# The layer-input gate as seven half-block products for each pair of token tiles

## Chip, cores and metric

The kernel runs on one core of a Trainium2 chip. The metric is device time in microseconds (us) of one execution: the median of several runs. A profile is one execution of its own, recorded by the hardware profiler; its span runs from the first instruction of the program to the last.

## What is computed

One layer of a streaming encoder in float32: 1024 prompt tokens and 8 x 16 sample tokens, which together are nine tiles of 128 tokens, with 1024 features each. Attention and the SwiGLU feed-forward come first and are not touched. The change concerns the end:

```python
    x = x + mix @ w_out
    h = rmsnorm(x, g_ffn)
    x = x + (jax.nn.silu(h @ w_gate) * (h @ w_up)) @ w_down      # w_down is 2816 x 1024
    gate = jax.nn.sigmoid(rmsnorm(x, g_ple) @ w_ple_gate)        # w_ple_gate is 1024 x 1024
    x = x + gate * (p @ w_ple_proj)
    return x, new
...
    y_prompt = rmsnorm(xp, g_final)
    y_sample = rmsnorm(xs, g_final)
```

The product `p @ w_ple_proj` is made much earlier and lies in DRAM (`proj`). The layer-input gate is the 1024 x 1024 product under the sigmoid.

## The kernel before, in words

**Numbers.** Each float32 operand is split in a high part (a cast to the matmul's reduced float32) and a low part (the difference). `mm3` makes one product of three matmuls: high by high, high by low, low by high. The cast is made by ACT, the difference by DVE or POOL (`sub`, L111). So 128 tokens by 128 features by n columns cost three matmuls of n columns.

**Queues and order.** Every DMA is issued by SP, in one in-order queue, in which an issue that waits holds up all behind it. The order of the instructions on each engine is made by the framework's scheduler; inside `tc.manual_schedule(engines=...)` an engine keeps the order in which the code is written.

**Down projection.** Ten of the eleven blocks of 256 rows of `w_down` are done in `nd = 5` iterations of 512 rows (`for d in range(nd)`). Tiles t and t + 4 form a pair; the two tiles by two halves of the features are a 2 x 2 block matrix, and `forms` makes the sums of blocks with which seven products do the work of eight. `raws(d)` loads an iteration's inputs one iteration ahead: `actr` (activations), `sr` (sums of activations, made earlier and kept in DRAM), `wr` and `wraw` (weights). `put` splits them in `acth`/`actl` (low part on POOL) and `whi`/`wlo` (low part on DVE); `plus` makes sums of weights (`t`, `wr`). `times` (L1307) is the products, `onto` (L1312) adds a bank of PSUM to the residual rows `x1[t]`. The eleventh block is left to `down`: for each tile t two halves of 512 columns, 12 matmuls, and an add (L1418). Before it, POOL adds twelve half rows `u2` onto `x1` (L1414).

**Gate.** `close(t)`, run after each tile's `down`, makes tile t's normalized row `hrow` (squares on ACT, L197; the power on POOL, L117; scaled by `g_ple` on DVE, L199), turns tile t - 1's row with eight transposes (L1452, out `pt`) and splits the result in `hVh` and `hVl`. `gate(c, w, t)` is one quarter of 256 columns for one tile: 24 matmuls of 256 columns (`mm3`, L106 to L108, out `ps` from `whi`/`wlo` and `hVh`/`hVl`), sigmoid (L1436), product with `pj` (L1437), add onto `x1` (L1438), squares for the last norm (L1439). Quarter 0 is interleaved with `down`; quarters 1 to 3 follow, each over nine tiles. In quarter 3 the final scale (L1479 to L1482) and the store of the tile follow. `wq`, `gated` and `wf` do not exist yet.

Of the kernel before, what the change touches and what calls it, by code (L numbers as in the profile page):

```python
# [13 lines left out]
F32 = mybir.dt.float32  # L14
F32R = mybir.dt.float32r
# [7 lines left out]
P = 128  # L23
D = 1024
# [15 lines left out]
def tile_hymba_step(  # L40
# [64 lines left out]
    def mm3(out, ah, al, bh, bl, start, stop):  # L105
        T.matmul(out, lhsT=ah, rhs=bh, start=start, stop=False)  # L106
        T.matmul(out, lhsT=ah, rhs=bl, start=False, stop=False)  # L107
        T.matmul(out, lhsT=al, rhs=bh, start=False, stop=stop)  # L108
# [48 lines left out]
    def cols(w, c, n=256):  # L157
        return w[:, c * n : (c + 1) * n].rearrange("(k p) c -> p k c", p=P)
# [50 lines left out]
    actd = [dram.tile([P, 2, NT * P], F32, name=f"act{i}") for i in range(DFF // 256)]  # L209
    actsd = [dram.tile([P, 3, 512], F32, name=f"acts{i}") for i in range(DFF // 256 - 1)]  # L210
    mixs = [dram.tile([P, 512], F32, name=f"mixs{i}") for i in range(2)]


    kv_prompt = {(0, 1): sb_k_p, (0, 2): sb_v_p, (1, 1): cb_k_p, (1, 2): cb_v_p}
# [504 lines left out]
    def pool(stack, name, side, bufs=1):  # L719
        return stack.enter_context(tc.tile_pool(name=name, bufs=bufs, side=side, reuse_waits="tile"))  # L720
# [243 lines left out]
    def bank(n=512):  # L964
        return ps_o.tile([P, 512], F32, name="ps", tag="O")[:, :n]
# [162 lines left out]
    with tc.tile_pool(name="ph4b", bufs=2, side="right", reuse_waits="tile") as p4b:  # L1128
# [200 lines left out]
    with tc.manual_schedule(engines={mybir.EngineType.SP}):  # L1329
        fetch_x1((0, 1, 2, 3, 8), 0)  # L1330
        fetch_x1((4, 5, 6, 7), 1)
        fetch_x1((0, 1, 2, 3, 8), 1)
        fetch_x1((4, 5, 6, 7), 0)
        ahead = raws(1)
    for d in range(nd):
# [68 lines left out]
    hT = Transposed()  # L1404
    for half in range(2):
        hT.add(pool(ctx, f"h5{half}", "left"), half, "hV")

    def down(w, act, last):
        for t in range(NT):
            s = slice(t * P, (t + 1) * P)  # L1410
            for half in range(2):
                o = slice(half * 512, half * 512 + 512)
                if t < NP and (t, half) > (3, 1) or t < 4 and half:
                    G.tensor_tensor(x1[t][:, o], x1[t][:, o], u2[t % 4], op=ALU.add)  # L1414
                ps_ = bank()
                for f in range(2):
                    mm3(ps_, act[f][0][:, s], act[f][1][:, s], w[0][:, f, o], w[1][:, f, o], f == 0, f == 1)
                V.tensor_tensor(x1[t][:, o], x1[t][:, o], ps_, op=ALU.add)  # L1418
            last(t)


    def gate_weights(c):
        return ch.load(cols(w_ple_gate[0], c), KT, 256, 2)

    p6 = pool(ctx, "ph6", "right", 2)
    ss = [p6.tile([P, 4], F32, name=f"ss{t}", bufs=1) for t in range(NT)]

    def gate(c, w, t):
        o = slice(c * 256, (c + 1) * 256)
        pj = p6.tile([P, 256], F32, name="pj", tag="pj", bufs=4)  # L1430
        nc.sync.dma_start(pj, proj[t * P : (t + 1) * P, o])
        ps_ = bank(256)
        for k in range(KT):
            mm3(ps_, *hT.tok(t, k), w[0][:, k], w[1][:, k], k == 0, k == KT - 1)
        sg = p6.tile([P, 256], F32, name="sgp", tag="sgp")
        A.activation(sg, ps_, AF.Sigmoid)  # L1436
        V.tensor_tensor(sg, sg, pj, op=ALU.mult)  # L1437
        (V if c == 3 else G).tensor_tensor(x1[t][:, o], x1[t][:, o], sg, op=ALU.add)  # L1438
        A.activation(sg, x1[t][:, o], AF.Square, accum_out=ss[t][:, c : c + 1])  # L1439

    def close(t):

        if t < NT:
            rows.append(normed(p6, x1[t], g_row, t))
        if t == 0:
            return
        h = rows.pop(0)
        for half in range(2):
            pt = tbank()
            for j in range(4):  # L1450
                c = (half * 4 + j) * P
                T.transpose(pt[:, j * P : (j + 1) * P], h[:, c : c + P], ident)  # L1452
            dh, dl = hT.dst(t - 1, half)
            A.copy(dh, four(pt))  # L1454
            sub(V, dl, four(pt), dh)
        if t > LATE:
            gate(0, w_g, t - 1 - LATE)

    w_g = gate_weights(0)
    g_row = load_row(gr, g_ple[0:1, :], "grow")  # L1460
    down(w_d, act, close)
    close(NT)
    for t in range(NT - LATE, NT):
        gate(0, w_g, t)


    gf_row = load_row(gr, g_final[0:1, :], "grow")
    for c in range(1, 4):
        w_g = gate_weights(c)
        for t in range(NT):  # L1470
            gate(c, w_g, t)
            if c == 2:
                part = p6.tile([P, 1], F32, name="part", tag="part", bufs=NT)
                V.tensor_reduce(part, ss[t][:, 0:3], axis=AX.X, op=ALU.add)
                V.tensor_scalar(ss[t][:, 0:1], part, 1.0 / D, EPS, op0=ALU.mult, op1=ALU.add)
                G.tensor_tensor(x1[t][:, :768], x1[t][:, :768], gf_row[:, :768], op=ALU.mult)
            if c == 3:
                r = p6.tile([P, 1], F32, name="r", tag="r", bufs=4)
                V.scalar_tensor_tensor(r, ss[t][:, 3:4], 1.0 / D, ss[t][:, 0:1], op0=ALU.mult, op1=ALU.add)  # L1479
                G.tensor_tensor(r, r, nhalf[:, 0:1], op=ALU.pow)  # L1480
                V.tensor_tensor(x1[t][:, 768:], x1[t][:, 768:], gf_row[:, 768:], op=ALU.mult)
                V.tensor_scalar(x1[t], x1[t], r[:, 0:1], None, op0=ALU.mult)  # L1482
                nc.sync.dma_start(y_tok[t], x1[t])


INPUTS = (
# [47 lines left out]
```

## Time and profile before

| | |
|---|---|
| median of 3 runs | 1732.53 us (1726.93 to 1733.93) |
| the profiled execution | 1727.71 us, its span 1725.6 us |
| busy share of the span | PE 97%, PEld 84%, DVE 61%, ACT 45%, POOL 45% |
| mean granted TensorE clock | 0.995 |
| stretch of the five iterations of the down projection | 1357 to 1571.5 us of the span |
| stretch of the last block, the transposes and the gate | 1571.5 to 1717.8 us |
| bytes moved by DMA | 279.40 MB |

How to read it: PE is TensorE's matmuls, PEld its weight loads, DVE VectorE, ACT ScalarE, POOL GpSimd, SPq the issue of a DMA by SP. A row of the timeline has the start in the span, the time taken, the engine, the line of the kernel, the operation, and "out<-in" by the program's names; in square brackets stands the idle time of the engine before it and who ended it. A row of groups has the count, the busy time of all, the mean of one in ns, and the idle time before them. A matmul's own duration is longer than the distance to the next one, since they overlap; a stretch and its count tell the rate. PEclk is the granted share of TensorE's clock.

### The profile page before, as it was taken

What the parts mean: (1) busy time and instruction counts of PE and PEld (TensorE: products, weight loads), DVE (VectorE), ACT (ScalarE), POOL (GpSimd) and SP (SyncE); (2) the same over time, 40 slices, a digit from 0 to 9 for tenths busy, and PEclk for the clock granted to TensorE, in tenths of its full rate; (3) what the DMA queues carried; (4) which work ended last, traced back from release to release, by engine and by line L of the source; (5) the groups of instructions that cost most, each with busy time, mean ns of one, the idle gap of its engine ahead of it and who ended that gap; (6) DMA issues with size and microseconds to landing.
All of it is one profiled execution on the core that took longest, in us unless ns stands there. A gap on an engine that the chain in (4) does not pass through costs nothing.

```text
span 1725.6 us, 29066 instructions
## 1 busy us (share of the span) xinstructions
PE 1668.2 (97%) x11076; PEld 1457.6 (84%) x11076; DVE 1044.9 (61%) x1640; ACT 776.4 (45%) x1698; POOL 774.3 (45%) x584
## 2 busy tenths in 40 slices
PE   8999999999997998899999999999999999999998
PEld 7998888889995887787778888888888788887998
DVE  5112344277778675654886666666666698887635
ACT  5214545276767776643643333333332343333432
POOL 2313301287446422222455555555554565558364
PEclk9999999999999999999999999999999999999999
DMA  5847898656469986855413222222222874311123
GB/s 191 278 145 226 287 293 284 189 171 184 119 176 267 296 252 185 232 165 176 142 56 115 88 87 90 95 95 95 95 95 95 291 292 136 120 39 61 59 71 141
DMA packets 172620, 279.40 MB, mean 162 GB/s; under 512 B 15297, under 2 KB 103617, under 8 KB 171074
## 3 DMA queue, kind: packets, MB, share of 16 engines
q1 hardware_dynamic: 172482, 277.55, 49.9%
q8 instruction: 88, 1.44, 0.4%
q14 instruction: 50, 0.41, 0.1%
HBM read 197.95 MB, written 79.56 MB: 161 GB/s over the span
## 4 chain that ended last, share of the span: by engine, by line
PE 86%; DMA 5%; DVE 3%; ACT 2%; issue 1%; POOL 1%; SPq 0%; POOLq 0%; ACTq 0%; DVEq 0%
PE ps L1056 20%; PE ps L106 9%; PE ps L107 9%; PE ps L108 9%; PE pt L1307 6%; PE ps L1307 4%; PE pt L1056 3%; PE pt L608 3%; PE pt L395 2%; PE po L632 2%; DMA mixn<-mixp 2%; PE acc L463 2%; PE po L631 2%; PE S L575 1%; PE sdec L418 1%; PE S L576 1%
## 5 line engine op out<-in xcount | busy, mean ns | idle before, releaser
L111 POOL TENSOR_TENSOR wlo<-wraw,whi 128x512 fp32r<-128x512 f32 (+1 forms) x127 | 224.4, 1794 | 205.6 <-ACT whi L150 201.7
L106 PE MATMUL ps<-whi,hTh 128*128 128x256 f32 x576 | 167.7, 291 | 0.1
L107 PE MATMUL ps<-wlo,hTh 128*128 128x256 f32 x576 | 164.2, 285 | 0.0
L108 PE MATMUL ps<-whi,hTl 128*128 128x256 f32 x576 | 163.9, 285 | 0.0
L150 ACT CAST whi<-wraw 128x512 fp32r<-128x512 f32 (+1 forms) x128 | 88.2, 753 | 94.1 <-PE ps L1056 64.8
L589 DVE TENSOR_TENSOR_SCAN keep<-keep,zero 128x128 f32<-128x128 f32 (+4 forms) x64 | 99.1, 1558 | 37.6 <-ACT keep L581 36.6
L590 POOL TENSOR_TENSOR w<-w,keep 128x127 f32<-128x127 f32 (+4 forms) x64 | 83.4, 1313 | 73.1 <-DVE keep L589 64.0
L106 PEld LDWEIGHTS ps<-whi,hTh 128*128 128x128 f32 x576 | 110.2, 191 | 6.0 <-issue 5.4
L108 PEld LDWEIGHTS ps<-whi,hTl 128*128 128x128 f32 x576 | 110.2, 191 | 0.5 <-DVE hTl L111 0.2
L107 PEld LDWEIGHTS ps<-wlo,hTh 128*128 128x128 f32 x576 | 110.3, 192 | 0.1
L111 DVE TENSOR_TENSOR wtl<-pt,wth 128x512 fp32r<-128x512 f32 (+1 forms) x192 | 94.2, 514 | 18.1 <-ACT wth L612 17.2
L612 ACT CAST wth<-pt 128x512 fp32r<-128x512 f32 (+1 forms) x192 | 84.4, 463 | 44.2 <-PE pt L608 43.4
L608 PE MATMUL pt<-ident,w 128*128 128x128 f32 x528 | 87.9, 278 | 5.5 <-POOL w L590 2.1
L106 PE MATMUL ps<-whi,hVh 128*128 128x256 f32 x288 | 81.9, 284 | 0.5 <-ACT hVh L1454 0.5
L107 PE MATMUL ps<-wlo,hVh 128*128 128x256 f32 x288 | 81.7, 284 | 0.0
L108 PE MATMUL ps<-whi,hVl 128*128 128x256 f32 x288 | 81.6, 284 | 0.0
L575 PE MATMUL S<-qk 128*128 128x384 f32 (+2 forms) x192 | 71.4, 373 | 5.8 <-ACT keep L581 3.9
L631 PE MATMUL po<-wth,vk 128*128 128x256 f32 (+1 forms) x304 | 76.3, 283 | 0.2
L608 PEld LDWEIGHTS pt<-ident,w 128*128 128x128 f32 x528 | 61.8, 141 | 15.4 <-issue 3.6
L632 PE MATMUL po<-wtl,vk 128*128 128x256 f32 (+1 forms) x304 | 72.7, 282 | 0.0
L111 POOL TENSOR_TENSOR actl<-actr,acth 128x1024 fp32r<-128x1024 f32 (+1 forms) x22 | 56.7, 2579 | 33.6 <-DMA sr<-acts 18.2
L106 PE MATMUL ps<-hTh,whi 128*128 128x384 f32 x192 | 66.0, 344 | 0.0
(359 smaller groups left out, 5335.9 us busy)
## 6 DMA issues: line engine op xcount, KB each, us to landing
draw<-in_cache_sb_k SPq DMA_DIRECT2D x32, 512.0 KB, 5.3
draw<-in_cache_sb_v SPq DMA_DIRECT2D x32, 512.0 KB, 5.1
act<-sg SPq DMA_DIRECT2D x11, 1152.0 KB
actr<-act SPq DMA_DIRECT2D x22, 576.0 KB, 5.4
wraw<-in_w_in SPq DMA_DIRECT2D x11, 1024.0 KB, 5.2
wraw<-in_w_gate SPq DMA_DIRECT2D x11, 1024.0 KB
wraw<-in_w_up SPq DMA_DIRECT2D x11, 1024.0 KB
v<-sv SPq DMA_DIRECT2D x36, 256.0 KB, 4.5
```

The lines of the kernel that those rows point to most:

```text
L106: T.matmul(out, lhsT=ah, rhs=bh, start=start, stop=False)
L107: T.matmul(out, lhsT=ah, rhs=bl, start=False, stop=False)
L108: T.matmul(out, lhsT=al, rhs=bh, start=False, stop=stop)
L111: eng.tensor_tensor(out, a, hi.bitcast(F32), op=ALU.subtract)
L150: A.copy(h[:, o], v[:, o])
L575: T.matmul(sc, lhsT=hd["qq"][:, qs], rhs=hd["kkh"][:, kc], start=True, stop=False)
L589: V.tensor_tensor_scan(rev, rev, zero[:, 0:1].to_broadcast([P, n]), 1.0, op0=ALU.mult, op1=ALU.add)
L608: T.transpose(pt[:, (c - c0) * P : (c - c0 + 1) * P], w[:, c * P : (c + 1) * P], ident)
L631: T.matmul(dst, lhsT=vs, rhs=wth[:, kb - base, c0:c1], start=(i == 0), stop=False)
L632: T.matmul(dst, lhsT=vs, rhs=wtl[:, kb - base, c0:c1], start=False, stop=(i == nkb - 1))
L1056: T.matmul(out, lhsT=a[x][:, k], rhs=b[y][:, k], start=(not more and k == 0 and n == 0), stop=(k == 3 and n == 2), skip_group_check=more)
L1307: T.matmul(out, lhsT=a[i][:, x, m * P : (m + 1) * P], rhs=b[j][:, x], start=(not more and x == 0 and n == 0), stop=(x == 1 and n == 2), sk ...
```

## The change

The gate's product is now made like the down projection's: for each pair (t, t + 4), A11, A12 are the halves of the features of tile t, A21, A22 those of tile t + 4, and seven products of half blocks (128 x 512 by 512 x 512 each) stand for eight. Tile 8, which has no partner, keeps the plain form. Parts:

- **Weights' sums beside the down projection.** `gate_sums(k)`, called in iterations d = 1 to 4 with k = d - 1, loads four 128 x 512 blocks of `w_ple_gate`, scales them by `g_ple` on ACT, makes four differences on POOL, and writes seven blocks to DRAM (`gated`). That is 16 loads, 16 ACT operations, 16 POOL operations and 28 stores of 256 KB.
- **Weights read back.** After the iterations, seven loads of 1 MB from `gated` go into the places of the buffers that the iterations leave (`wf`) and are split in place (`weights_parts`): W0, W2, W4 and the seventh with their low parts on DVE, W1, W3, W5 on POOL.
- **Tiles in the order** 0, 4, 1, 5, 2, 6, 3, 7, 8 in `down`; the twelve POOL adds stand ahead of them all.
- **`prepare(p)`** makes a pair's rows (no `g_ple` any more; scaled on ACT, on DVE for tiles 0, 4 and 8; one buffer `hrow` instead of two), turns them, and makes the sums and seven splits. PE's order from here to the end is written out by hand.
- **The pair loop**: seven products (12 matmuls of 512 columns each), into four banks, with adds on DVE (`u`, `u3`, `u4`), and four gates of 512 columns. Then tile 8 by 24 matmuls of 512 and 72 of 256 columns.
- `proj` comes in two rows of 1024 per pair in place of 36 loads of 256 columns; the final scale is one DVE operation on 1024 columns with both factors.

```diff
-    xr, gr = pool(ctx, "xr", "right"), pool(ctx, "gr", "right")
+    xr = pool(ctx, "xr", "right")
...
+    def gate_sums(k):
+
+        q = {}
+        for x in range(2):
+            for y in range(2):
+                q[x, y] = wq.tile([P, 512], F32, name=f"q{x}{y}", tag=f"q{x}{y}", bufs=1)
+                row = (x * 4 + k) * P
+                nc.sync.dma_start(q[x, y], w_ple_gate[0, row : row + P, y * 512 : y * 512 + 512])
+                A.activation(q[x, y], q[x, y], AF.Copy, scale=g_gate[:, x * 4 + k : x * 4 + k + 1])
...
+        for i, v in ((0, q[0, 0]), (1, q[1, 0]), (6, q[1, 1])):
+            out(i, v)
+        G.tensor_tensor(t3, q[1, 1], q[0, 1], op=ALU.subtract)
+        G.tensor_tensor(q[0, 1], q[0, 1], q[0, 0], op=ALU.subtract)
+        G.tensor_tensor(t2, q[1, 1], q[0, 1], op=ALU.subtract)
+        G.tensor_tensor(q[1, 0], q[1, 0], t2, op=ALU.subtract)
+        for i, v in ((2, t2), (3, t3), (4, q[0, 1]), (5, q[1, 0])):
+            out(i, v)
...
         S3, T3, A4, T4 = got
+        if d:
+            gate_sums(d - 1)
...
+    W = [own_place(i) for i in range(5)] + [ch.pair(4, 512)]
+    for i in range(6):
+        nc.sync.dma_start(W[i][1].bitcast(F32), gated[i])
+    b22 = ch.raw(gated[6], 4, 512)
...
-    def gate(c, w, t):
-        o = slice(c * 256, (c + 1) * 256)
...
-        for k in range(KT):
-            mm3(ps_, *hT.tok(t, k), w[0][:, k], w[1][:, k], k == 0, k == KT - 1)
...
+    weights_parts(0, V)
+    weights_parts(2, V)
+    for i, t in enumerate(tiles):
+        down(t, w_d, act)
+        if i == 1:
+            coming = prepare(0)
+            next(coming)
+            with tc.issue_after(pows[0].ins):
+                weights_parts(1, G)
+        if i == 4:
+            next(coming)
+            weights_parts(3, G)
+            weights_parts(5, G)
+        if i == 6:
+            forms_ = next(coming)
+            with tc.issue_after(last_split[0]):
+                weights_parts(4, V)
+    W.append(ch.parts(b22, 4, 512, 2, V))
...
+    for p in range(4):
+        A11, A12, S2, S3, S1, A22, S4 = forms_
...
+        product(a, A11, W[0])
+        A.copy(u, a)
...
+        product(b, S2, W[2])
+        V.tensor_tensor(u, u, b, op=ALU.add)
+        product(a, A12, W[1], True)
...
+        product(c, S3, W[3])
+        V.tensor_tensor(u3, u, c, op=ALU.add)
+        if p < 3:
+            next(coming)
...
+            gate(p, 0, 512, 0, a, G)
...
+        product(d, S1, W[4])
+        V.tensor_tensor(u3, u3, d, op=ALU.add)
+        gate(p + 4, 512, 512, 1, u3, G)
+        if p < 3:
+            forms_ = next(coming)
+        product(c, A22, W[5], True)
+        V.tensor_tensor(u4, u, c, op=ALU.add)
+        gate(p + 4, 0, 512, 0, u4, G)
+        close(p + 4, 2)
+        product(d, S4, W[6], True)
+        V.tensor_tensor(u, u, d, op=ALU.add)
+        gate(p, 512, 512, 1, u, G)
+        close(p, 2)
```

How this moves instructions, at three places. Line numbers after the change are those of the changed kernel: L1223 has become L1224, L1231 L1232, L1273 L1274, L1056 (`product`) L1057.

**SP, the loads for the fourth iteration of the down projection.** Before, these stand one behind the other (`actr` is that iteration's activations, `wraw` and `wr` its weights):

```order
L1223 DMA actr<-act_105 128x1152
L1223 DMA actr<-act_106 128x1152
L135 DMA wraw<-in_w_down 128x2x1024
L1223 DMA actr<-act_105 128x1152
L1223 DMA actr<-act_106 128x1152
L1231 DMA wr<-in_w_down 128x2x1024
```

And now (L1348 is a load of `gate_sums`, L1353 a store; `gated_120` to `gated_126` are the seven blocks):

```order
L1224 DMA actr<-act_105 128x1152
L1224 DMA actr<-act_106 128x1152
L1353 DMA gated_122<-t_16374 128x512
L1348 DMA q_16700<-in_w_ple_gate 128x512
L1348 DMA q_16706<-in_w_ple_gate 128x512
L1353 DMA gated_120<-q_16697 128x512
L135 DMA wraw<-in_w_down 128x2x1024
L1353 DMA gated_125<-q_16368 128x512
L1224 DMA actr<-act_105 128x1152
L1224 DMA actr<-act_106 128x1152
L1353 DMA gated_126<-q_16706 128x512
L1232 DMA wr<-in_w_down 128x2x1024
```

Four DMAs of `gate_sums` now stand between the first `actr` pair and `wraw`, one between `wraw` and the second pair, one between that and `wr`; each store waits for the ACT or POOL operation that makes its block.

**POOL, in the third iteration.** Before, from the first low part of that iteration's sums on:

```order
L111 TENSOR_TENSOR actl<-sr,acth 128x1024 x2
L1273 TENSOR_TENSOR t_15679<-wraw,t_15679 128x1024
L111 TENSOR_TENSOR actl<-sr,acth 128x1024
L111 TENSOR_TENSOR actl<-actr,acth 128x1024
L1273 TENSOR_TENSOR wr<-wraw,wr 128x2x512
L111 TENSOR_TENSOR actl<-actr,acth 128x1024 x3
```

Now, from one row further on (L1357 to L1360 are the differences of `gate_sums`):

```order
L1360 TENSOR_TENSOR q_16020<-q_16020,t_16026 128x512
L111 TENSOR_TENSOR actl<-sr,acth 128x1024
L1274 TENSOR_TENSOR t_15713<-wraw,t_15713 128x1024
L1357 TENSOR_TENSOR t_16375<-q_16371,q_16365 128x512
L111 TENSOR_TENSOR actl<-sr,acth 128x1024
L1358 TENSOR_TENSOR q_16365<-q_16365,q_16362 128x512
L111 TENSOR_TENSOR actl<-actr,acth 128x1024
L1359 TENSOR_TENSOR t_16374<-q_16371,q_16365 128x512
L1274 TENSOR_TENSOR wr<-wraw,wr 128x2x512
L1360 TENSOR_TENSOR q_16368<-q_16368,t_16374 128x512
L111 TENSOR_TENSOR actl<-actr,acth 128x1024 x2
```

The scheduler put the differences together: of the 16, counted from one iteration's last `d8l` to the next one's, 4 stand in the second iteration's list, 11 in the third's, 1 in the fourth's, none in the fifth's.

**PE, the gate.** Before, quarter 0 of the gate (`hV`, 256 columns), the last block's `down` (`act`, 512 columns) and the transposes stand mixed:

```order
L106 MATMUL ps<-whi,hVh_16701 128x256
L1452 MATMUL pt<-ident,hrow 128x128 x8
L107 MATMUL ps<-wlo,hVh_16701 128x256
L108 MATMUL ps<-whi,hVl_16702 128x256
L106 MATMUL ps<-whi,hVh_16701 128x256
```

Now each pair has its products of 512 columns, with the next pair's transposes ahead of and behind the product with W4 (its twelve matmuls are rows like the three shown):

```order
L1057 MATMUL ps<-W3h,actl 128x512
L1500 MATMUL pt<-ident,hrow 128x128 x8
L1057 MATMUL ps<-W4h,acth 128x512
L1057 MATMUL ps<-W4l,acth 128x512
L1057 MATMUL ps<-W4h,actl 128x512
```

After W4's twelve matmuls come the eight transposes of the pair's second tile. Both sets read the same single buffer `hrow`, so twelve matmuls lie between them.

More of the change, by code (lines that the diff above doesn't have):

```diff
@@ L211, in tile_hymba_step @@
     mixs = [dram.tile([P, 512], F32, name=f"mixs{i}") for i in range(2)]
+    gated = [dram.tile([P, 4, 512], F32, name=f"gated{i}") for i in range(7)]
     kv_prompt = {(0, 1): sb_k_p, (0, 2): sb_v_p, (1, 1): cb_k_p, (1, 2): cb_v_p}
@@ L1401, in tile_hymba_step @@
             onto(4 + m, 0, m7[m])
-    bstack.close()
[L1404 to L1419, printed above, removed]
@@ L1441, in close @@
[L1441 to L1449, printed above, removed]
-            for j in range(4):
[L1451 to L1483, printed above, removed]
@@ new lines, in tile_hymba_step, with weights_parts @@
+    tiles = [0, 4, 1, 5, 2, 6, 3, 7, 8]
+    for t in tiles[:-1]:
+        for half in range(2):
+            if t > 3 or half:
+                o = slice(half * 512, half * 512 + 512)
+                G.tensor_tensor(x1[t][:, o], x1[t][:, o], u2[t % 4], op=ALU.add)
+    bstack.close()
+    wf = pool(ctx, "wf", "left")
+    def weights_parts(i, eng):
+        hi, lo = W[i]
+        raw_ = lo.bitcast(F32)
+        for o in (slice(0, 2), slice(2, 4)):
+            A.copy(hi[:, o], raw_[:, o])
+            sub(eng, lo[:, o], raw_[:, o], hi[:, o])
@@ new lines, in own_place, with down @@
+    def own_place(i):
+        return [wf.tile([P, 4, 512], F32R, name=f"W{i}{n}") for n in "hl"]
+    W = [own_place(i) for i in range(5)] + [ch.pair(4, 512)]
+    for i in range(6):
+        nc.sync.dma_start(W[i][1].bitcast(F32), gated[i])
+    b22 = ch.raw(gated[6], 4, 512)
+    def down(t, w, act):
+        s = slice(t * P, (t + 1) * P)
+        for half in range(2):
+            o = slice(half * 512, half * 512 + 512)
+            ps_ = bank()
+            for f in range(2):
+                mm3(ps_, act[f][0][:, s], act[f][1][:, s], w[0][:, f, o], w[1][:, f, o], f == 0, f == 1)
+            V.tensor_tensor(x1[t][:, o], x1[t][:, o], ps_, op=ALU.add)
@@ new lines, in tile_hymba_step, with squares @@
+    p6 = pool(ctx, "ph6", "right")
+    ss = [p6.tile([P, 4], F32, name=f"ss{t}", bufs=1) for t in range(NT)]
+    def squares(t, place):
+        s_ = p6.tile([P, 2], F32, name="s_n", tag="s_n", bufs=3)
+        for i in range(2):
+            A.activation(place, x1[t][:, i * 512 : i * 512 + 512], AF.Square, accum_out=s_[:, i : i + 1])
+        r = p6.tile([P, 1], F32, name="r_n", tag="r_n", bufs=3)
+        V.tensor_scalar(r, s_[:, 0:1], s_[:, 1:2], 1.0 / D, op0=ALU.add, op1=ALU.mult)
+        V.tensor_scalar(r, r, EPS, None, op0=ALU.add)
+        pows[:] = [G.tensor_tensor(r, r, nhalf[:, :1], op=ALU.pow)]
+        return r
@@ new lines, in scaled, with turned_tile @@
+    def scaled(t, r):
+        h = p6.tile([P, D], F32, name="hrow", tag="hrow", bufs=1)
+        if t % 4:
+            A.activation(h, x1[t], AF.Copy, scale=r[:, 0:1])
+        else:
+            V.tensor_scalar(h, x1[t], r[:, 0:1], None, op0=ALU.mult)
+        return h
+    pows, last_split = [], []
+    def turned_tile(h):
+        pt = [four(tbank()) for _ in range(2)]
+        for i in range(2):
+            for j in range(4):
+                T.transpose(pt[i][:, j], h[:, (i * 4 + j) * P : (i * 4 + j + 1) * P], ident)
+        return pt
@@ new lines, in tile_hymba_step, with gate @@
+    turn = [0]
+    def gate(t, lo, n, i, src, eng):
+        o = slice(lo, lo + n)
+        turn[0] = 1 - turn[0]
+        sg = sA.tile([P, 2, 2, P], F32R, name="sgp", tag="d8" + "hl"[turn[0]], bufs=1)
+        sg = sg.bitcast(F32).rearrange("p a b c -> p (a b c)")[:, :n]
+        A.activation(sg, src, AF.Sigmoid)
+        V.tensor_tensor(sg, sg, proj_in[t][:, o], op=ALU.mult)
+        eng.tensor_tensor(x1[t][:, o], x1[t][:, o], sg, op=ALU.add)
+        A.activation(sg, x1[t][:, o], AF.Square, accum_out=ss[t][:, i : i + 1])
@@ new lines, in tile_hymba_step @@
+    h8 = [[v[:, i * 4 : i * 4 + 4] for v in last8] for i in range(2)]
+    for i, (lo, n) in enumerate(((0, 512), (512, 256), (768, 256))):
+        out = bank(n)
+        cut = slice(lo % 512, lo % 512 + n)
+        terms = ((0, 0), (1, 1)) if lo == 0 else ((0, 0), (0, 4), (1, 6))
+        for j, (half, f) in enumerate(terms):
+            for k in range(4):
+                mm3(out, h8[half][0][:, k], h8[half][1][:, k], W[f][0][:, k, cut], W[f][1][:, k, cut],
+                    j == 0 and k == 0, j == len(terms) - 1 and k == 3)
+        gate(NP, lo, n, i, out, V)
```

88 lines of the change are left out of this document (77 added, 11 removed).

## The prediction

> **What bounds the kernel now.** I read the page's busy shares first, then stretches by time, then the chain and PE's waits in the part that changes.
>
> ```profile
> PE 1668.2 (97%) x11076; PEld 1457.6 (84%) x11076; DVE 1044.9 (61%) x1640; ACT 776.4 (45%) x1698; POOL 774.3 (45%) x584
> 1440.90:1484.40 43.50, 43.50 (x194) 36.02 (x193) 35.11 (x41) 15.68 (x18) 24.09 (x11) 1.00 0.42 139
> 1571.50:1717.80 146.30, 143.63 (x1068) 137.58 (x1067) 80.29 (x146) 57.12 (x149) 77.80 (x70) 0.99 0.23 78
> 1580.20:1600.00 19.80, 17.74 (x96) 15.62 (x95) 15.28 (x24) 9.72 (x17) 9.90 (x9) 0.91 0.16 53
> 1600.00:1640.00 40.00, 39.47 (x290) 37.27 (x289) 24.84 (x39) 19.93 (x48) 13.76 (x15) 1.00 0.21 66
> 1640.00:1717.80 77.80, 77.72 (x648) 77.51 (x646) 33.87 (x76) 27.47 (x85) 45.44 (x40) 1.00 0.28 99
> ```
>
> The columns are the stretch, its length, busy time and count of PE, PEld, DVE, ACT and POOL, PE's granted clock, DMA share and GB/s. PE is the bound in both parts that are touched: never idle in an iteration of the down projection, and idle 2.6 us of the last 146.3. The counts give its rates. An iteration has 192 matmuls of 512 columns (seven products of 4 x 2 x 3, and 24 for tile 8; two more straddle the edges): 43.5 / 192 = 0.2267 us each. Quarters 1 to 3 of the gate are 3 x 9 x 24 = 648 matmuls of 256 columns in 77.8 us: 0.12 us each. So work on PE is what counts, as long as the others keep up.
>
> **The sum, part by part.** First PE's work from 1571.5 us on.
>
> ```profile
> L106 PE MATMUL ps<-whi,hVh 128*128 128x256 f32 x288 | 81.9, 284 | 0.5 <-ACT hVh L1454 0.5
> L1307 PE MATMUL pt<-whi,acth 128*128 128x512 f32 x8 | 3.1, 389 | 0.0
> 1600.93 0.87 PE pt L1452 x8
> 1589.87 3.32 PE L1452 MATMUL pt<-ident,hrow 128*128 128x128 f32 x16 [2.06 <-DVE hrow L199]
> ```
>
> Before: 3 x 288 = 864 gate matmuls x 0.12 = 103.7; the fifth iteration's remainder, 3 x 8, and `down`'s 9 x 12 matmuls of 512 columns, 132 x 0.2267 = 29.9; nine times eight transposes x 0.87 = 7.8; together 141.4. The 4.9 that are missing to 146.3 are 2.6 of waiting and about 2 of the lower clock at 1580 to 1600. After: 7 products x 12 x 4 pairs + 24 = 360 matmuls of 512 columns = 81.6, and 72 of 256 = 8.6: 90.2 in place of 103.7. `down`, the remainder and the transposes stay as they are: 127.9. The product count falls by an eighth for eight tiles of nine, which is where **13.5 us** come from; wider matmuls add next to nothing.
>
> What of the 4.9 comes back? The row with 16 transposes shows a wait of 2.06 for `hrow`, followed by transposes at 0.21 each in place of 0.11, and the stretch around it has a clock of 0.91: 0.09 x 19.8 = 1.8 more. I allow 3 us for waits in the transition and in the pair loop (bounds 0 and 8, below). By the Trainium skill (TensorE: Matmul & The Clock Gate, Part 1) the clock falls after a window of about 3.4 us without work; by that rule a wait of 2.06 would cost itself alone, 2.1, by the row it costs 3.9. The row decides, and my 3 is under one such wait.
>
> *The transition.* The weights' places come free late:
>
> ```profile
> 1567.37 2.68 POOL L111 TENSOR_TENSOR actl<-actr,acth 128x1152 fp32r<-128x1152 f32 x1
> 1570.01 13.26 POOL L1414 TENSOR_TENSOR x<-x,v 128x512 f32<-128x512 f32 x9
> L111 POOL TENSOR_TENSOR wlo<-wraw,whi 128x1024 fp32r<-128x1024 f32 x8 | 19.3, 2432 | 1.5 <-ACT whi L150 1.5
> wraw<-in_w_in SPq DMA_DIRECT2D x11, 1024.0 KB, 5.2
> ```
>
> W1's place is `actr`'s, which POOL reads until 1570.05; the others follow until PE leaves the fifth iteration at about 1580. At 5.2 us to land, and even one behind the other, six loads are in by about 1605, and the first product starts at 1571.5 + 29.9 + 16 transposes (1.7) = 1603.1; W5, the last, is wanted 15 us later. POOL ends its adds at 1583.3, then W3, W1, W5 take 3 x 2 x 2.43 = 14.6 and wait once for ACT's casts: to about 1601, wanted from 1608.5 on. POOL's powers for tiles 4 and 1 stand behind W3 and W1: tile 4's row is then ready at about 1593 and its transposes are due at 1596.7. So the slack is 4 us and more everywhere; I cost the transition at the allowance above. If a link slips past its slack, PE waits for the rest of it in full: upper bound 8.
>
> *The pair loop.* PE per pair: 84 x 0.2267 + 16 x 0.109 = 20.8 us. The others, by rows:
>
> ```profile
> L1454 ACT CAST hVh<-pt 128x512 fp32r<-128x512 f32 x18 | 9.8, 586 | 11.1 <-PE pt L1452 11.0
> L197 ACT ACTIVATE hrow<-x 128x1024 f32<-128x1024 f32 x9 | 9.5, 1061 | 1.3 <-DVE x L1418 1.3
> L1436 ACT ACTIVATE sgp<-ps 128x256 f32<-128x256 f32 x36 | 13.9, 386 | 33.1 <-PE ps L108 32.8
> L111 DVE TENSOR_TENSOR hVl<-pt,hVh 128x512 fp32r<-128x512 f32 x18 | 12.0, 686 | 4.0 <-ACT hVh L1454 3.9
> L1437 DVE TENSOR_TENSOR sgp<-sgp,pj 128x256 f32<-128x256 f32 x36 | 23.2, 647 | 38.1 <-ACT sgp L1436 37.9
> L199 DVE SCALAR_TENSOR_TENSOR hrow<-x,r_n,row_grow 128x1024 f32<-128x1024 f32 x9 | 12.4, 1384 | 0.9 <-POOL r_n L117 0.9
> ```
>
> ACT: 9 casts and copies x 0.59, 2 rows x 1.06, 4 sigmoids at about 0.6, 8 squares of 512 with their sums at about 0.8: 16.2. DVE: 12 operations on PSUM x 0.69, 4 products of 512 at 0.7 to 1.2, 2 last scales x 1.38, ten small ones at 0.15: 16.3. POOL: 3 splits and 4 adds at 1.3 to 1.6, 4 powers x 0.6: 13. All are under 20.8, so PE stays the bound. The narrowest place is `hrow` with its one buffer: between the two sets of transposes PE has 12 x 0.2267 = 2.7 us, in which ACT must make two casts and the row, 0.59 + 0.59 + 1.06 = 2.2 with the first cast begun early. Of the next pair's sums, s2's split is due 2.7 us into the next pair, with 2 to 3 us to spare.
>
> *The sums beside the down projection.* 16 ACT scalings at about 0.6 hide in ACT's 28 idle us an iteration. 16 POOL differences and 45 DMAs do not hide as well:
>
> ```profile
> 1460.41 2.42 POOL L111 TENSOR_TENSOR actl<-actr,acth 128x1024 fp32r<-128x1024 f32 x1
> 1461.15 2.77 DVE L111 TENSOR_TENSOR wlo<-wraw,whi 128x1024 fp32r<-128x1024 f32 x1 [0.46 <-ACT whi L1266]
> 1464.44 1.21 DVE L111 TENSOR_TENSOR wlo<-wr,whi 128x1024 fp32r<-128x1024 f32 x1
> L111 POOL TENSOR_TENSOR d8l<-actr,d8h 128x256 fp32r<-128x256 f32 x2 | 1.4, 741 | 0.5 <-ACT d8h L1288 0.5
> 1470.54 0.80 SPq L1223 DMA_DIRECT2D actr<-act  x2
> 1475.36 0.38 SPq L1231 DMA_DIRECT2D wr<-in_w_down  x1
> 1476.14 1.06 ACT L1266 CAST acth<-actr 128x1024 fp32r<-128x1024 f32 x1 [2.48 <-issue]
> 1480.35 2.00 ACT L1266 CAST whi<-wr 128x1024 fp32r<-128x1024 f32 x2
> 1481.69 1.22 DVE L111 TENSOR_TENSOR wlo<-wr,whi 128x1024 fp32r<-128x1024 f32 x1
> 1484.45 0.91 PE ps L1307 x4
> v<-sv SPq DMA_DIRECT2D x36, 256.0 KB, 4.5
> ```
>
> A DVE split takes 1.21 alone; beside POOL's operation that ends at 1462.83 it takes 2.77, to 1463.92, which is POOL's end and a full operation after it. The two take turns. 1024 columns cost POOL 2.42 and 256 cost 0.74, so 512 cost about 1.3. The third iteration gets 11 of them: 14.3 on top of POOL's 24.1, of 43.5; DVE has ten operations that take turns with POOL's, about 11.6. The three make 50, more than 43.5, and the rest slides into the fourth, which has room again (24.1 + 1.3 + 11.6). The `actl` that POOL makes are wanted 10 us and more after they are ready, so a slide of 6.5 us is hidden there. What isn't: the fourth iteration's second `actr` pair waits for POOL's last low part of the third, goes out perhaps 5 us later than at 1470.54, and the cast that waits for it (1476.14) stands ahead of the weights' casts (1480.35) and low parts (1481.69) that PE wants at 1484.45. That chain has some 4 us of play. On the queue, 2.75 MB for each sum, three sums, come on top of 139 GB/s there: 8.25 MB / 43.5 us = 190 GB/s more. Lower bound 0 (the play suffices); upper bound 8 (the slide of 6.5 and a landing later by 4.5, less part of the play). I take **2.5**, nearer the lower, since the play is of the size of the delay. The first, second and fifth iterations I cost at nothing: few or no differences.
>
> *The end.*
>
> ```profile
> 1717.82 0.39 ACT sgp L1436
> 1719.69 0.42 ACT sgp L1439
> 1721.16 0.76 DVE x L1482
> ```
>
> After the last matmul the chain keeps its steps; the square's sum is reduced and scaled by two small DVE operations in place of one (0.15), and the last scale of 1024 columns has two tensor inputs, 1.2 to 1.4 (the row of `hrow`) in place of 0.76: **+0.6** (0.3 to 1).
>
> Sum against the profiled execution, 1727.71 us: 127.9 + 3 in place of 146.3 is -15.4; +2.5 and +0.6: **-12.3**, 1715.4. The median of the runs, 1732.53, is 4.8 above that execution; the same difference gives **1720**.
>
> **Rivals.** *Slower: the sums' stores hold up the down projection.* Now SP's queue has stores that wait for POOL ahead of the loads that POOL, ACT and PE live on, and POOL's last difference of each sum waits for a store. Where the play of 4 us is gone, each late load goes to PE in full. If the port's turns (16 x 1.3 = 21 us, all of it) and one landing of 4.5 at each of three boundaries came out as PE waits, 34 in place of 2.5: 1751. It decides from about 23 us lost in the iterations on, where slower by 0.5% begins. Against it: it needs waits in iterations that get 4 differences or 1. The Trainium skill (SBUF — State Buffer, Who interferes with whom) says that a DVE instruction with two SBUF inputs and a GpSimd one that reads SBUF block each other for the whole instruction. By that rule, the trace agrees: 2.77 against 1.21.
>
> *Same: the pair loop waits for its rows.* With one `hrow`, every set of transposes waits as the one did at 1589.87: seven sets in the loop x 2.1 = 14.7 in place of the 3 allowed: 1720.2 + 11.7 = 1732. For it: the row; ACT is strictly in order and its gate squares wait for POOL, with a row behind them. Against it: that wait came while POOL still had its adds and splits to do, and 2.2 is under 2.7.
>
> *The whole gain and more:* no wait at all, 1720.2 - 5.5 = 1714.7; part of my likeliest case.
>
> **Chances.** Likeliest case 0.67, its own range 1713 to 1726; same by the pair loop 0.20; slower by the iterations 0.11; anything else 0.02. A change under 0.5% (8.7 us) can't be told from none here. Of the second case some ends half way and is still faster: faster 0.69, same 0.20, slower 0.11. The range takes in no wait at all, less 4 for the scatter of the medians (1726.93 to 1733.93), and above the second case whole: 1711 to 1734.
>
> **What would show it.** Right: PE without waits and 192 matmuls per 43.5 us in the first, second and fifth iterations; at most 5 us of PE waits at the start of the fourth; the pair loop at 20.8 to 21.5 us a pair; the last matmul 12 to 18 us earlier than 1717.8. Wrong: PE waits on `whi` or `wlo` of L1267 in several iterations, PE waiting at L1500 for `hrow` in each pair, or products waiting for W1, W3 or W5.

## The result, and the profile after

The changed kernel takes 1721.18 us (median of 4 runs, 1720.26 to 1721.93); the kernel before 1732.09 (4 runs). The ratio is 0.9942, with a 95% interval of 0.9928 to 0.9956: about 10 us faster, of which the interval allows 7.6 to 12.5. The profiled execution took 1720.26, its span is 1718.4. A few runs took far longer (one of number 1 below at 4184.91 us, two of the kernel before at 2347.20 and 4208.02), and the medians and ratios here are of the others.

The busy shares of the whole program, then stretches (stretch, its length, busy time and count of PE, PEld, DVE, ACT, POOL, PE's clock, DMA share, GB/s):

```profile
PE 1661.6 (97%) x10644; PEld 1435.4 (84%) x10644; DVE 1069.8 (62%) x1646; ACT 803.2 (47%) x1713; POOL 809.0 (47%) x590
1442.90:1486.40 43.50, 40.28 (x173) 32.72 (x173) 29.49 (x34) 19.79 (x26) 37.01 (x18) 0.96 0.73 254
1477.80:1492.50 14.70, 11.48 (x39) 8.67 (x39) 9.73 (x9) 7.62 (x10) 12.18 (x6) 0.77 0.99 359
1579.70:1710.35 130.65, 129.14 (x636) 108.00 (x634) 99.39 (x153) 74.30 (x148) 80.16 (x60) 1.00 0.30 116
1580.00:1610.00 30.00, 28.59 (x132) 22.85 (x131) 25.49 (x38) 18.95 (x32) 26.63 (x17) 1.00 0.50 207
1610.00:1694.00 84.00, 84.00 (x401) 70.16 (x400) 66.27 (x103) 49.93 (x103) 49.29 (x40) 1.00 0.24 88
```

Before, PE had no wait from 1400 us to 1587; now it idles for 3.2 at the end of the third iteration (first two stretches: 43.50 less 40.28, 14.70 less 11.48), and the clock is down there. The pair loop (last row) has none. To place the time, the same matmul is looked up in both traces: the first `d8` matmul of iteration 2 and, three iterations on, that of iteration 5. They serve as markers. Before:

```profile
1413.57 0.39 PE L106 MATMUL ps<-whi,d8h 128*128 128x512 f32 x1
1544.13 0.39 PE L106 MATMUL ps<-whi,d8h 128*128 128x512 f32 x1
```

After:

```profile
1415.52 0.39 PE L106 MATMUL ps<-whi,d8h 128*128 128x512 f32 x1
1552.31 0.39 PE L106 MATMUL ps<-whi,d8h 128*128 128x512 f32 x1
```

So this execution was 2.0 us behind when it came to the iterations, and 8.2 behind in the fifth: the iterations lost **6.2 us**. The 2.0 are not the change's: they are there at 1391 us already, and the first load of `gate_sums` goes out at 1395.2. (In the other profiles below the first marker stands at 1413.0 to 1419.5: executions scatter by that much.) All of the 6.2 lies in one place of the third iteration, the product S3 by T3, the sixth of the seven in the code's order. PE's waits in the part that changed:

```profile
1482.79 0.57 PE L1308 MATMUL pt<-whi,acth 128*128 128x512 f32 x1 [1.83 <-ACT whi L1267]
1484.75 0.79 PE L1308 MATMUL pt<-wlo,acth 128*128 128x512 f32 x1 [1.39 <-DVE wlo L111]
1597.51 0.50 PE L106 MATMUL ps<-whi,acth 128*128 128x512 f32 x1 [1.16 <-DVE x L1469]
1599.36 0.50 PE L106 MATMUL ps<-whi,acth 128*128 128x512 f32 x1 [0.20 <-DVE x L1469]
```

The two waits of the iterations make 3.2 us; the other 3.0 are the clock, 0.77 over 14.7 us (0.23 x 14.7 = 3.4, of which a part falls on the second wait). The chain that ended last shows what the first wait hung on, link by link:

```profile
1471.64 1.30 POOL t L1359
1472.96 0.32 SPq L1353
1473.37 0.55 SPq L1348
1473.97 6.46 DMA q<-in_w_ple_gate
...
1481.08 0.72 ACT q L1349
1481.80 0.94 ACT whi L1267
1482.77 1.94 DVE wlo L111
```

POOL makes a difference; SP's queue has a store of it (L1353) ahead of two loads of `w_ple_gate` (L1348); these take 6.5 us to land; ACT's scaling (L1349) waits for them; the cast of the down projection's weights stands behind the scaling in ACT's order. DVE's low part then takes 1.9 in place of 1.2, beside POOL.

From the fifth iteration's remainder to the last matmul it is 130.65 us (1579.70 to 1710.35), against 146.3 before: **15.65 us won**. The pair loop's pace is seen in the chain by the first set of transposes in each of its four passes, 20.83 to 20.85 us apart:

```profile
1624.62 0.87 PE pt L1500 x8
...
1645.45 0.87 PE pt L1500 x8
...
1666.30 0.87 PE pt L1500 x8
...
1687.13 0.87 PE pt L1500 x8
```

At the end the last scale takes 1.28 in place of 0.76, and from the last matmul (1710.35) to the end of the span it is 8.05 us, against 7.8: 0.25 lost. The same chain:

```profile
1710.35 0.39 ACT sgp L1561
...
1713.59 1.28 DVE x L1572
```

Sum of the profiled executions: 2.0 + 6.2 - 15.65 + 0.25 = -7.2, the difference of the spans. Without the 2.0, which lie ahead of the change, it is -9.2; the medians say -10.9, with the interval above.

### The profile page after: what moved, and what is told of

It reads as the page before. It is cut to its first block, busy times and chain, and to the rows that moved or that the text cites. A ratio compares the mean times of both kernels' runs of the same rounds, so it can differ in the third digit from the quotient of the medians.

```text
span 1718.4 us, 28232 instructions
## 1 busy us (share of the span) xinstructions
PE 1661.6 (97%) x10644; PEld 1435.4 (84%) x10644; DVE 1069.8 (62%) x1646; ACT 803.2 (47%) x1713; POOL 809.0 (47%) x590
## 4 chain that ended last, share of the span: by engine, by line
PE 85%; DMA 5%; DVE 4%; ACT 3%; issue 1%; POOL 1%; SPq 1%; POOLq 0%; ACTq 0%; DVEq 0%
PE ps L1057 24%; PE ps L106 8%; PE ps L107 7%; PE ps L108 7%; PE pt L1308 6%; PE ps L1308 4%; PE pt L1057 3%; PE pt L609 3%; PE pt L396 2%; PE po L633 2%; PE S L576 2%; PE acc L464 2%; PE po L632 1%; PE sdec L419 1%; PE S L577 1%
## 5 line engine op out<-in xcount | busy, mean ns | idle before, releaser
L111 POOL TENSOR_TENSOR wlo<-wraw,whi 128x512 fp32r<-128x512 f32 (+1 forms) x119 | 204.9, 1749 | 203.5 <-ACT whi L150 203.5
L150 ACT CAST whi<-wraw 128x512 fp32r<-128x512 f32 (+1 forms) x122 | 82.1, 739 | 81.7 <-PE ps L1057 66.1
L111 POOL TENSOR_TENSOR actl<-actr,acth 128x1024 fp32r<-128x1024 f32 (+1 forms) x22 | 60.5, 2753 | 27.1 <-DMA sr<-acts 18.2
L397 DVE COPY kT<-pt 128x512 f32<-128x512 f32 x48 | 33.0, 688 | 53.4 <-PE pt L396 49.4
L108 PE MATMUL ps<-hTh,wlo 128*128 128x384 f32 x192 | 65.7, 342 | 0.0
L107 PE MATMUL ps<-hTl,whi 128*128 128x384 f32 x192 | 65.3, 340 | 0.0
```

The lines of the kernel that those rows point to most:

```text
L111: eng.tensor_tensor(out, a, hi.bitcast(F32), op=ALU.subtract)
```

## Experiments

Two losses are left to explain: 6.2 us in the iterations and about 2 in the transition, and one gain to price. A ratio is to the kernel before, run in the same session; the changed kernel's is 0.9942.

**1. No differences.** In `gate_sums`, the scaled blocks themselves are stored in place of the four differences:

```diff
-        G.tensor_tensor(t3, q[1, 1], q[0, 1], op=ALU.subtract)
...
-        G.tensor_tensor(q[1, 0], q[1, 0], t2, op=ALU.subtract)
-        for i, v in ((2, t2), (3, t3), (4, q[0, 1]), (5, q[1, 0])):
+        for i, v in ((2, q[1, 1]), (3, q[0, 0]), (4, q[0, 1]), (5, q[1, 0])):
```

> The changed kernel with the sixteen POOL differences of gate_sums left out: blocks 2 to 5 are stored as the scaled blocks themselves; loads, ACT scalings and stores stay. In the changed kernel PE loses 6.2 us at the end of the third iteration (waits of 1.8 and 1.4 and a lowered clock behind them). Theory Q (queue chain: a store on SP waits for a POOL difference, the next loads of w_ple_gate stand behind that store, ACT's scaling waits for those loads, and the cast of the down projection's weights stands behind the scaling): stores no longer wait for POOL, PE's wait at the end of the third iteration is gone, 6.2 us less, about 1715. Theory P (POOL is overfull and takes turns with DVE): also gone, 1715. Theory M (the extra 11.5 MB of traffic make the weights late): the loss stays, 1721.

**2. No scalings.** The changed kernel without this line, and without the small load of `g_gate` that only it reads:

```diff
-                A.activation(q[x, y], q[x, y], AF.Copy, scale=g_gate[:, x * 4 + k : x * 4 + k + 1])
```

> The changed kernel with ACT's sixteen scalings by g_ple left out: the POOL differences, all loads and all stores stay. Theory Q: nothing on ACT waits for a load of w_ple_gate any more, so the weights' cast can start when POOL's t3 difference is done (1475.3 in the changed kernel's profile) and PE's wait is gone: about 1715. Theory P: POOL has the same 16 differences beside DVE, the wait stays at 3 us and the loss near 6: about 1721. Theory M: 1721.

Measured: 1714.65 us without differences (ratio to the kernel before 0.9904, 0.9891 to 0.9918) and 1716.04 without scalings (0.9908, 0.9894 to 0.9922). Between the two marker matmuls the first takes 130.56 us, exactly as before the change; the second 1.06 more, by a wait of 0.77 for a bank in iteration 4. The third iteration's stretch, without differences and then without scalings:

```profile
1442.00:1486.00 44.00, 44.00 (x196) 36.45 (x195) 35.86 (x41) 21.61 (x27) 25.02 (x11) 1.00 0.86 298
```

```profile
1442.00:1486.00 44.00, 44.00 (x196) 36.44 (x195) 36.18 (x40) 15.81 (x18) 38.20 (x19) 1.00 0.76 251
```

The first has all the traffic (298 GB/s, more than the changed kernel's 254) and PE waits for nothing: traffic alone is out. The second has POOL busy for 38.2 us of 44, with its differences beside DVE, and PE waits for nothing either: POOL's load and its turns with DVE are out as the cause of the loss. Each takes away a link of the chain above. Without scalings nothing on ACT waits for a load of `w_ple_gate`. Without differences ACT still has a scaling that waits for such a load ahead of the cast, but the stores ahead of that load no longer wait for POOL: the load goes out at 1467.32, the scaling starts at 1474.59 in place of 1481.08, and PE is not kept waiting. This is theory Q. The same two waits stand in the profiles of numbers 4, 6 and 8 below, which leave the iterations as they are (6.8, 5.6 and 5.6 us lost between the markers).

**3. Loads held back** behind the loads of the iteration's own sums (`sums_in`), for the last sum behind those of the last block's activations (`last_in`):

```diff
...
-            gate_sums(d - 1)
+            with tc.issue_after((sums_in[d + 1, 1] if ahead else last_in).ins):
+                gate_sums(d - 1)
```

> The changed kernel with each sum's loads held on SP behind the loads of the iteration's own sums (for the last sum, behind the last block's activations), so that the third iteration gets 7 to 8 POOL differences in place of 11 and the last sum runs in the fifth iteration, where the DMA share was 0.07. Nothing is left out. Theory Q: loads of w_ple_gate stand ahead of the stores that wait for POOL and land before ACT comes to the scaling; PE's wait at the end of the third iteration is gone or under 1 us: 1715 to 1716. Theory P: with 7 to 8 x 1.3 = 10 us more on POOL instead of 14.3 the loss is about two thirds: 1719. Theory M: traffic in that iteration falls by a third, 1719.

Measured: 1714.30 (0.9907, 0.9894 to 0.9921), with runs from 1713.07 to 1718.89. The profiled one, the slowest, still shows the chain's end: three of the loads stand ahead of the stores now, but one, issued at 1472.22, takes about 8 us, ACT scales at 1480.38, the weights' cast follows, and PE waits once. The clock stayed up this time, and the loss between the markers is 2.0 us:

```profile
1472.22 0.43 SPq L1350 DMA_DIRECT2D q<-in_w_ple_gate  x1
1480.38 0.72 ACT L1351 ACTIVATE q<-q,g_gate 128x512 f32<-128x512 f32 x1 [4.62 <-DMA q<-in_w_ple_gate]
1481.95 1.04 ACT L1269 CAST whi<-wr 128x1024 fp32r<-128x1024 f32 x1
1483.04 1.21 PE L1310 MATMUL pt<-whi,acth 128*128 128x512 f32 x4 [1.66 <-ACT whi L1269]
```

So in this execution it is not the store ahead of the load as such, but a load that is late while ACT's scaling stands ahead of the cast. (The other runs are 1.5 to 5.8 us shorter; whether they have this wait is not shown.)

**4. A buffer of its own for the squares** (aimed at the transition):

```diff
-        place = u2[3 * (1 - (p + 1) % 2)]
+        place = u2[3 * (1 - (p + 1) % 2)] if p else p6.tile([P, 512], F32, name="s4", tag="s4", bufs=1)
```

> The changed kernel with a buffer of its own for the discarded squares of tiles 0 and 4 (in the changed kernel they are written to u2[0], which POOL's adds still read until about 1589.6). Only ACT's first square moves, ahead of the first W casts. Theory: the chain into PE's waits of 1.2 and 0.2 us at 1597 (DVE idle for r_n, ACT's squares, POOL's adds) starts about 2.4 us earlier and both waits go, 1.5 to 2.5 us less: about 1719. Rival: the waits come from DVE's splits of W2 and from hrow, which stand ahead of the adds that free PSUM and wait for POOL's power behind its adds anyway: no change, 1721. Neither theory touches the loss of 6.2 us at the end of the third iteration.

A miss, in both theories: 1725.41 (0.9966, 0.9953 to 0.9979), slower than the changed kernel by 4 us. The profiled execution, the slowest, reaches iteration 5 at 1556.83 in place of 1552.31, so 4.5 has to be taken off its times; from there to the last matmul it takes 162.6 us, the changed kernel 158.0. The row of tile 0 came about 1 us earlier, as expected, and with it DVE's splits of W2, which now ran beside POOL's splits of W3. First the changed kernel's rows:

```profile
1595.64 1.22 DVE L111 TENSOR_TENSOR W2l<-W2l,W2h 128x1024 fp32r<-128x1024 f32 x1
1597.37 1.22 DVE L111 TENSOR_TENSOR W2l<-W2l,W2h 128x1024 fp32r<-128x1024 f32 x1
1597.36 3.49 POOL L111 TENSOR_TENSOR W3l<-W3l,W3h 128x1024 fp32r<-128x1024 f32 x1 [2.19 <-ACT W3h L1451]
1600.80 2.41 POOL L111 TENSOR_TENSOR W3l<-W3l,W3h 128x1024 fp32r<-128x1024 f32 x1
```

With the squares' own buffer:

```profile
1598.94 3.41 DVE L111 TENSOR_TENSOR W2l<-W2l,W2h 128x1024 fp32r<-128x1024 f32 x1
1602.87 2.79 DVE L111 TENSOR_TENSOR W2l<-W2l,W2h 128x1024 fp32r<-128x1024 f32 x1
1598.85 2.42 POOL L111 TENSOR_TENSOR W3l<-W3l,W3h 128x1024 fp32r<-128x1024 f32 x1 [0.38 <-ACT W3h L1451]
1603.00 0.50 PE L106 MATMUL ps<-whi,acth 128*128 128x512 f32 x1 [2.46 <-DVE x L1469]
1606.42 0.80 PE L106 MATMUL ps<-whi,acth 128*128 128x512 f32 x1 [1.26 <-DVE x L1469]
```

In both kernels a split of DVE meets one of POOL. In the changed kernel DVE's keeps its 1.22 and POOL's takes 3.49 in place of 2.41; here POOL's keeps 2.42 and DVE's takes 3.41, and the add that frees PE's bank stands behind it. The start times, POOL's ahead by 0.01 us there and by 0.09 here, are too close to tell the two cases apart. The Trainium skill (SBUF — State Buffer, Who interferes with whom) says that a DVE instruction with two SBUF inputs contends with a GpSimd one that reads SBUF, and that the order of issue decides which of the two is blocked. These rows agree: one runs at its own time, and the other pays. PE's waits are 3.7 us in place of 1.4, and behind them the clock is 0.91 from 1578 to 1618, where it was 1.00 in the changed kernel.

**5. Scalings behind the casts.** `cast_` is the last cast of the next iteration's first weights:

```diff
-        A.copy(hi, src)
+        cast_[:] = [A.copy(hi, src)]
...
-        if d:
-            gate_sums(d - 1)
         if ahead is not None:
             now = forms(ahead)
             got = next(now)
+            with tc.issue_after(cast_[0].ins):
+                gate_sums(d)
```

> The changed kernel with each sum's ACT scalings held behind the cast of the next iteration's first weights (the last cast before ACT's idle time at an iteration's start), one sum in each of the iterations 2 to 5, four POOL differences each. Nothing is left out. Theory Q: no scaling that waits for a load stands ahead of a weights' cast any more; PE has no wait in the iterations, the loss of 6.2 us is gone: 1714 to 1715, without the spread to 1719 that the sums with held-back loads showed. Rival M: the loads, now issued well ahead among the iteration's own loads, make those late in the second iteration, where the DMA share is 0.8 to 0.9: PE waits there, 1717 to 1720.

Measured: 1714.95 (0.9914, 0.9896 to 0.9932; 1712.94 to 1715.73). Between the markers 130.56 us: nothing is lost, with all loads, scalings, differences and stores in place. Rival M is out. The edit changes more than ACT's order, though: the loads go out earlier and land before the scalings come (no scaling waits for one), and the third iteration gets 4 differences in place of 11. So it does not tell which of the two, the new order or the earlier loads, would do alone. Its transition happens to be worse (161.9 from the second marker to the last matmul), since there too one split of W2 met POOL's W3:

```profile
1589.29 3.44 DVE L111 TENSOR_TENSOR W2l<-W2l,W2h 128x1024 fp32r<-128x1024 f32 x1
1589.26 2.38 POOL L111 TENSOR_TENSOR W3l<-W3l,W3h 128x1024 fp32r<-128x1024 f32 x1 [2.18 <-ACT W3h L1453]
1593.50 0.50 PE L106 MATMUL ps<-whi,acth 128*128 128x512 f32 x1 [2.42 <-DVE x L1471]
```

**6. W2 late**, and **7. both edits together** (`rows_[0]` is the operation that makes tile 4's row):

```diff
...
-    weights_parts(2, V)
...
             next(coming)
+            with tc.issue_after(rows_[0].ins):
+                weights_parts(2, V)
             weights_parts(3, G)
```

> The changed kernel with DVE's two splits of W2 held behind tile 4's row, so that they no longer stand between the adds that free PSUM for down's products at 1595 to 1598. Theory T (PE's waits of 1.2 and 0.2 us come from DVE's order, W2's splits and the row ahead of an add): both waits go, 1.4 to 2 us less, 1719 to 1720. Rival: the splits meet POOL's splits of W3 and W1 at the new place, take about 3 in place of 1.22 us each, as they did with the squares' own buffer, and PE waits later for a bank or for W2: no change or up to 4 us more.

> The two edits of the runs beside it together: scalings behind the casts, and W2's splits behind tile 4's row. If the two losses are apart from each other: the sum of the two differences, 1712 to 1713 by theories Q and T; 1714 to 1718 where W2's splits meet POOL's.

Measured: 1724.93 (0.9974, 0.9960 to 0.9987) and 1718.76 (0.9941, 0.9923 to 0.9960). Number 6 is the rival's mechanism, at its upper end or past it (slower than the changed kernel by 3.7 us by the medians, by 5.5 by the ratios): the waits at the old place are gone, and one of 3.8 us stands at the new one, behind two splits of 3.4 us each:

```profile
1599.48 6.14 POOL L111 TENSOR_TENSOR W3l<-W3l,W3h 128x1024 fp32r<-128x1024 f32 x2
1599.99 6.70 DVE L111 TENSOR_TENSOR W2l<-W2l,W2h 128x1024 fp32r<-128x1024 f32 x2
1607.35 0.80 PE L106 MATMUL ps<-whi,acth 128*128 128x512 f32 x1 [3.85 <-DVE x L1469]
```

Number 7, just above its expected 1714 to 1718, has no loss in the iterations (130.56 us between the markers) and the same wait in the transition. By the ratios numbers 5 and 6 are 0.0028 below and 0.0032 above the changed kernel, together 0.0004; number 7 is at -0.0001. So the two losses are apart from each other.

**8. One product more per pair.**

```diff
         product(d, S4, W[6], True)
+        product(d, S4, W[6], True)
```

> The changed kernel with the last product of each pair made a second time (12 matmuls of 512 columns more per pair, 48 in all; it adds that product twice). It prices one of the eight products that the change saves. If PE alone bounds the pair loop: 48 x 0.2267 = 10.9 us more, 1732, the time of the kernel before without the change of form. If other engines or the rows' buffer were near the bound, PE's extra time would be hidden in part: 3 to 8 us more.

Measured: 1730.68 (1.0006, 0.9994 to 1.0018), 0.0064 of the kernel before's time or 11 us above the changed kernel (9.5 by the medians), where 10.9 was expected. In the chain, the first set of transposes of two passes:

```profile
1623.79 0.87 PE pt L1500 x8
...
1647.35 0.87 PE pt L1500 x8
```

23.56 us apart in place of 20.84: 2.72 = 12 x 0.2267. PE alone bounds the pair loop, and a product saved is worth its whole time.

**9. Scalings behind the casts, and W2 early**, beside POOL's adds and ahead of its splits (`w2_cast` is ACT's last cast of W2, `pows` are the powers of tiles 0 and 4, `sq_[1]` is tile 0's last square):

```diff
...
-    weights_parts(2, V)
+    w2_cast = weights_parts(2, V)
...
             coming = prepare(0)
-            next(coming)
-            with tc.issue_after(pows[0].ins):
+            with tc.issue_after(w2_cast.ins):
+                next(coming)
+            with tc.issue_after(pows[1].ins), tc.issue_after(sq_[1].ins):
                 weights_parts(1, G)
...
-            weights_parts(3, G)
-            weights_parts(5, G)
+            with tc.issue_after(pows[0].ins):
+                weights_parts(3, G)
+                weights_parts(5, G)
```

> The kernel with the scalings behind the casts, and W2 split early in place of late: ACT casts W2 right after W0 (while it waits for POOL's adds anyway), so that DVE's two splits of W2 stand ahead of tile 0's row, beside POOL's adds, and not beside POOL's splits of W3. Nothing is left out. Theory T2 (DVE's split of W2 takes 1.2 us alone, 1.7 beside an add of 512 columns, 3.4 beside a split of 1024 on POOL; PE's waits for PSUM at the transition are that difference): the waits of 1.2 and 2.4 us go, 1711 to 1712. Rival (PE waits for DVE's order as such, wherever W2 stands): waits of 2 to 4 us stay in the transition, 1714 to 1716.

Measured: 1713.06 (0.9888, 0.9871 to 0.9905), the best of all. The waits for PSUM are gone; the splits of W2 took 2.1 and 1.7 beside adds. What PE waits for now is the rows, of which one is made beside W3:

```profile
1592.62 5.20 POOL L111 TENSOR_TENSOR W3l<-W3l,W3h 128x1024 fp32r<-128x1024 f32 x2
1592.69 2.87 DVE L1494 TENSOR_SCALAR hrow<-x,r_n 128x1024 f32<-128x1024 f32 x1
1595.62 1.09 PE L1503 MATMUL pt<-ident,hrow 128*128 128x128 f32 x8 [1.16 <-DVE hrow L1494]
1602.73 1.09 PE L1503 MATMUL pt<-ident,hrow 128*128 128x128 f32 x8 [0.55 <-DVE hrow L1494]
```

The expected 1711 to 1712 was 1 us off: 3.6 us of waits became 1.7, not 0. Its time can't be told from number 5's (the intervals overlap). In the traces the waits differ, and the way from the second marker to the last matmul is 157.9 us against 161.9 in number 5. The changed kernel's is 158.0: in these executions number 9 mends what number 5 had lost in the transition, and its gain over the changed kernel is that of the iterations.

## Why the prediction was right, and where not

- **The whole:** 1720 against 1721.18, faster as forecast. By the traces the sum is -9.2 in place of -12.3; the medians differ by -10.9. The 1.7 between the two lie inside the interval, and nothing here tells them from scatter. So it is luck in part that the median came within 1.2 us of the forecast: by the traces the gain is 3.1 short, for 3.7 more were lost in the iterations than forecast, and 0.25 and 0.35 less in the tail and at the end. The sign that the last matmul would come 12 to 18 us earlier than 1717.8 failed: it came 7.45 earlier, or 9.4 without the 2.0 that lie ahead of the change.
- **PE's work in the tail:** 127.9 and an allowance of 3, 130.9; measured 130.65. 20.8 us a pair was 20.84. Of the 15.65 won, 13.5 are the products by the prediction's count, and number 8 shows that a product is worth its full time; the other 2.15 are waits and clock, 2.75 in place of 4.9.
- **The allowance:** the first product of a pair starts at 1613.6; 1603.1 shifted by 8.2 is 1611.3, so the transition took 2.3 of the 3. The waits came from a place that was not on the prediction's list: not a row, a weight or a power, but the adds that free PSUM, behind DVE's splits. That the slack was 4 us everywhere did not hold: tile 4's row, forecast 3.7 ahead of its transposes, was ready at 1606.66 for transposes at 1607.23, 0.6 ahead (POOL's adds ended at 1595.2, where 1583.3 and the 8.2 make 1591.5). And in numbers 4 to 7, where a DVE split paid for POOL's, PE waited 3.6 to 3.9 us in place of 1.4.
- **The pair loop's rival** (same time, each set of transposes waits for the one `hrow`) did not happen: no wait in seven sets. By the row from 1610 to 1694 DVE, ACT and POOL are busy for 16.4, 12.4 and 12.2 us a pair; 16.3, 16.2 and 13 were forecast.
- **The sums beside the down projection, the step that failed:** predicted 2.5 (0 to 8), measured 6.2. The place is the product S3 by T3 of the third iteration, one product ahead of the boundary that was named. The 16 scalings were costed at nothing because ACT has 28 idle us in an iteration. Numbers 1, 2 and 5 together show that they were the link, with the late loads behind POOL's stores: idle time does not help when an instruction that waits for a load stands ahead of the one that PE needs. The chain that the prediction named instead (the second `actr` pair late, its cast ahead of the weights' casts) was half there: the pair went out at 1478.92, 6.4 later than 1470.54 moved by 2.0, but it cost nothing. Its cast stands where it stood, behind the casts of T3 and T4, which were late themselves, and ahead of those of the fourth iteration's first weights; ACT came to it at 1483.59 without idling, and PE had no wait at the boundary. POOL's turns with DVE, which the slower rival also counted on, cost 0.7 in the one low part.
- **The clock:** the prediction priced a wait of 2.06 at 3.9 in the transition, and left this out of the iterations' term. There 3.2 us of waits cost 6.2: of the miss of 3.7, the waits make 0.7 and the clock 3.0.
- **The end:** +0.6 predicted, +0.25 measured.

## To carry to other kernels

Work that is put beside a full engine must be costed by where it stands in each in-order queue, not by the idle time of its engine: ask of each added instruction what it may wait for, and what stands behind it. Holding it behind the instruction that the bound engine needs, with its loads issued earlier (number 5), took the whole loss away and left out nothing. And where DVE and POOL both split operands, starts less than 0.1 us apart can end either way, and DVE's split then takes 1.2 us or 3.4; look for such meetings before and after each reordering.

## What was not expected of the hardware

- Moving an operation earlier made the kernel slower (number 4). Of a DVE and a POOL split of 128 x 1024 that start within 0.1 us of each other, one took its time alone and the other paid: POOL's in the changed kernel (3.49 for 2.41 us), DVE's in numbers 4 and 5 (3.41 and 3.44 for 1.22).
- Two waits of 1.83 and 1.39 us within 2 us of each other were followed by a clock of 0.77 over 14.7 us and cost 6.2 us; one of 1.66 (number 3) was not, and cost 2.0. In number 6 waits of 2.04 and 1.46 cost 5.6, with a shorter time at the low clock (0.83 from 1480 to 1484, 0.74 to 1488).
- In the changed kernel a load of 256 KB of `w_ple_gate` took 6.5 to 8.1 us to land, with 7.3 as the median, at a DMA share of 0.7 to 0.99, against the median of 4.5 that the prediction took from the loads of `v`, of the same size.
